# A four-layer hybrid encoder on one core: new layouts of input and result, one transfer for the small tensors, a new order in the first layer

## The chip, the cores and the metric

The kernel runs on 1 core of one Trainium2 chip. The metric is the device time of one execution in microseconds (us). Before the change the median of 3 runs is 1135.5 us (1133.83 to 1135.89).

A core has a matrix engine (TensorE: PE for its products, PEld for its weight loads), VectorE (DVE), ScalarE (ACT), GpSimd (POOL) and SyncE (SP), which only issues transfers here. Each engine works through its own instructions in a fixed order and waits for the others by semaphores. 16 DMA engines move the data; transfers are issued on the queue of SP or of ACT.

## The reference

x has 256 tokens of 1024 values. Four layers follow, each of them a token mixer and a squared-ReLU MLP with 4096 hidden values, each with an RMSNorm ahead of it and a residual sum behind it. Layers 0 and 3 mix by a diagonal complex state-space model (S5) with a gate, layer 1 by differential attention, layer 2 by pooling.

```python
for i in range(DEPTH):
    kind, j = i % N_MIXERS, i // N_MIXERS
    h = rmsnorm(x, norm_mix[i])
    if kind == 0:
        m = s5_mixer(h, s5_w_in[j], s5_lam_re[j], s5_lam_im[j], s5_log_step[j], s5_b_re[j], s5_b_im[j],
                     s5_c_re[j], s5_c_im[j], s5_d[j], s5_w_gate[j], s5_w_out[j])
    ...
    x = x + m.astype(x.dtype)
    h = rmsnorm(x, norm_mlp[i])
    x = x + sqrelu_mlp(h, mlp_w1[i], mlp_w2[i]).astype(x.dtype)
return rmsnorm(x, norm_final).astype(x.dtype)
```

The S5 mixer of a layer: u = h w_in; in each of 64 groups a recurrence over the tokens with 64 complex states, whose coefficients come from lam, step, b and c; y from the states plus d u; z = gelu(y); z times sigmoid(z w_gate); the product with w_out.

## The kernel before

The 256 tokens are two tiles (t = 0, 1) of 128 partitions; x stays in the on-chip memory for the whole run (start_x_1, start_x_2). Partition p of tile t holds token 128 t + 4 (p mod 32) + p // 32: four tokens that follow each other form a step of the recurrence, and their place s in the step is the slowest part of the partition's number. So the view of x and of the result in DRAM is "(t c s) d -> t s c d", with s = 4 outermost.

All weights come as 338 blocks of 128 x 1024 values in the order of their use (`load`, three buffers named raw). In most products a block is split into a rounded high part and a low part (whi by ScalarE, wlo by VectorE), and three products take the place of one. The first layer's input product (w_in) and the first of its gate blocks take the block as it is, in full precision.

In `s5` of layer 0 the order of the work is written by hand: SEQ[0] is a list of steps, each a letter and a number, and all engines keep to it. The letters that matter here:

- p: the parameters (dt, mag, a sine, the factors wa, wb, pa, pb), in seven pieces, small steps of VectorE, with copies on ScalarE for wb, pa and pb.
- f q t: transpose block q of x in tile t on TensorE, copy it out on ScalarE times the norm's weights (`first`). x: the norm's statistics (ScalarE, then GpSimd).
- g n: a quarter of the input product, 8 matrix products in full precision with one block of weights for one half of the input; V n reads it out and transposes it on VectorE.
- i, I, d, o, O, s, a, r: tables of a quarter (products of the coefficients s5bc with the factors on VectorE, copies on ScalarE); S: four transposes of the table; T, U: a small table from 16 products. Z: GpSimd clears a table.
- m, n, c, C, y, z: states in, transposition, recurrence on VectorE in two parts, output product and GELU, transposition of the quarter.
- e and w: the gate and the output product. From the last transposition (z) on the order of both versions is the same.

At the start (`build`) ScalarE's queue issues the unit matrix and the norm weights (ident, cols), SP's queue the parameters of the first layer (prm), x in four transfers of 256 KB, the first two blocks of weights, the first half of the coefficients (in_s5bc) and three small tensors (dskip, chunk, gmask). At most eight transfers are open: each later one waits until the one eight places ahead of it has landed.

At the end (`last`), for each tile, the second half of x gets the final norm: ScalarE sums squares, GpSimd makes 1/rms, ScalarE or VectorE scales, and SP stores the half row (line 1239).

## Time and profile before

| | before |
|---|---|
| median of 3 runs | 1135.5 us (1133.83 to 1135.89) |
| the profiled execution | 1133.78 us |
| its span, first to last instruction | 1132.0 us |
| TensorE busy | 1091.0 us (96%) |
| VectorE busy | 792.5 us (70%) |
| ScalarE busy | 661.6 us (58%) |
| GpSimd busy | 57.9 us (5%) |
| moved by DMA | 196.50 MB, mean 174 GB/s |

The span counts from the first to the last instruction; what the time has beyond it (1.8 us) lies around the execution. The rows below come from this one execution. In a timeline each row is a run of like instructions of one engine: start, duration, engine, line, operation, result <- operands, and in brackets how long the engine stood idle before it and what it waited for. A helper records most instructions, so that nearly all of them have line 106; they are told apart by their tiles. One product of full precision leaves two records.

### The profile page before, as it was taken

What the parts mean: (1) busy time and instruction counts of PE and PEld (TensorE: products, weight loads), DVE (VectorE), ACT (ScalarE), POOL (GpSimd) and SP (SyncE); (2) the same over time, 40 slices, a digit from 0 to 9 for tenths busy, and PEclk for the clock granted to TensorE, in tenths of its full rate; (3) what the DMA queues carried; (4) which work ended last, traced back from release to release, by engine and by line L of the source; (5) the groups of instructions that cost most, each with busy time, mean ns of one, the idle gap of its engine ahead of it and who ended that gap; (6) DMA issues with size and microseconds to landing.
All of it is one profiled execution on the core that took longest, in us unless ns stands there. A gap on an engine that the chain in (4) does not pass through costs nothing.

```text
span 1132.0 us, 18755 instructions
## 1 busy us (share of the span) xinstructions
PE 1091.0 (96%) x7128; PEld 965.0 (85%) x7128; DVE 792.5 (70%) x1464; ACT 661.6 (58%) x1314; POOL 57.9 (5%) x113
## 2 busy tenths in 40 slices
PE   5989999999999999999999999999998999999994
PEld 4878798999887888999898899988897889899883
DVE  8997699567668987967655865565569777555653
ACT  4797576556665676666545754454473366444542
POOL 2301010000010011000000200000010001000000
PEclk9999999999999999999999999999999999999997
DMA  5314477766664535667667366666655565666561
GB/s 160 113 38 125 155 198 235 231 196 220 198 183 147 167 113 186 209 201 216 189 190 231 95 190 187 184 183 189 186 167 150 164 189 172 194 188 186 174 190 51
DMA packets 56698, 196.50 MB, mean 174 GB/s; under 512 B 7200, under 2 KB 7712, under 8 KB 56608
## 3 DMA queue, kind: packets, MB, share of 16 engines
q1 hardware_dynamic: 54560, 189.70, 55.9%
q10 hardware_dynamic: 2048, 5.61, 1.4%
q8 instruction: 56, 0.92, 0.3%
q14 instruction: 34, 0.28, 0.1%
HBM read 188.46 MB, written 6.82 MB: 173 GB/s over the span
## 4 chain that ended last, share of the span: by engine, by line
PE 87%; DVE 7%; ACT 2%; DMA 2%; issue 1%; SPq 0%; POOL 0%; DVEq 0%; ACTq 0%; POOLq 0%
PE mlp_ps L169 65%; PE mix_ps L169 21%; DVE mix_m L106 6%; PE mix_ps L173 2%; DMA start_raw<-in_wts 1%; ACT start_T L106 1%; ACT mix_m L106 1%; ACT mlp_m L106 0%; PE mlp_ps L173 0%; DMA mix_raw<-in_wts 0%; DVE mix_wlo L106 0%; ACT mix_whi L106 0%; SPq L1139 0%; DVE mix_mx L106 0%; DVE mix_cad L106 0%
## 5 line engine op out<-in xcount | busy, mean ns | idle before, releaser
L106 DVE TENSOR_TENSOR mlp_wlo<-mlp_raw,mlp_whi 128x512 fp32r<-128x512 f32 x492 | 319.1, 687 | 216.2 <-ACT mlp_whi L106 215.9
L106 ACT CAST mlp_whi<-mlp_raw 128x512 fp32r<-128x512 f32 x492 | 282.1, 619 | 257.6 <-PE mlp_ps L169 201.8
L169 PE MATMUL mlp_ps<-mlp_whi,mlp_m 128*128 128x512 f32 x1024 | 327.8, 396 | 0.0
L169 PEld LDWEIGHTS mlp_ps<-mlp_whi,mlp_m 128*128 128x128 f32 x1024 | 192.8, 188 | 45.5
L169 PE MATMUL mlp_ps<-mlp_m,mlp_whi 128*128 128x256 f32 x1248 | 226.2, 283 | 0.0
L169 PE MATMUL mlp_ps<-mlp_wlo,mlp_m 128*128 128x512 f32 x512 | 202.9, 396 | 0.0
L169 PEld LDWEIGHTS mlp_ps<-mlp_m,mlp_whi 128*128 128x128 f32 x1248 | 192.1, 188 | 0.6
L169 PE MATMUL mlp_ps<-mlp_m,mlp_wlo 128*128 128x256 f32 x624 | 175.2, 281 | 0.0
L169 PE MATMUL mlp_ps<-mix_m,mlp_whi 128*128 128x256 f32 x672 | 122.1, 283 | 0.0
L169 PEld LDWEIGHTS mlp_ps<-mlp_m,mlp_wlo 128*128 128x128 f32 x624 | 118.3, 190 | 0.0
L169 PEld LDWEIGHTS mlp_ps<-mlp_wlo,mlp_m 128*128 128x128 f32 x512 | 96.5, 188 | 22.1
L169 PE MATMUL mix_ps<-mix_whi,mix_m 128*128 128x512 f32 (+1 forms) x352 | 106.6, 379 | 0.0
L169 PEld LDWEIGHTS mlp_ps<-mix_m,mlp_whi 128*128 128x128 f32 x672 | 104.5, 188 | 1.8
L106 DVE TENSOR_TENSOR mix_wlo<-mix_raw,mix_whi 128x512 fp32r<-128x512 f32 x124 | 80.8, 687 | 29.8 <-ACT mix_whi L106 29.7
L106 ACT CAST mix_whi<-mix_raw 128x512 fp32r<-128x512 f32 x124 | 71.8, 621 | 47.0 <-PE mix_ps L169 22.9
L169 PE MATMUL mlp_ps<-mix_m,mlp_wlo 128*128 128x256 f32 x336 | 94.5, 281 | 0.0
L169 PEld LDWEIGHTS mix_ps<-mix_whi,mix_m 128*128 128x128 f32 x352 | 64.3, 188 | 13.7 <-issue 0.9
L169 PE MATMUL mix_ps<-mix_wlo,mix_m 128*128 128x512 f32 (+1 forms) x176 | 66.0, 375 | 0.0
L106 DVE TENSOR_TENSOR mlp_m<-mlp_m,mlp_m 128x512 fp32r<-128x512 f32 (+1 forms) x72 | 51.7, 718 | 19.4 <-ACT mlp_m L106 19.3
L169 PEld LDWEIGHTS mlp_ps<-mix_m,mlp_wlo 128*128 128x128 f32 x336 | 63.8, 190 | 0.0
L106 ACT CAST mlp_m<-mlp_m 128x512 fp32r<-128x512 f32 x64 | 39.8, 622 | 23.0 <-DVE mlp_m L106 22.7
L106 DVE TENSOR_TENSOR mix_m<-mix_m,mix_m 128x512 f32<-128x512 f32 (+3 forms) x64 | 44.8, 727 | 5.6 <-ACT mix_m L106 4.9
(307 smaller groups left out, 1378.2 us busy)
## 6 DMA issues: line engine op xcount, KB each, us to landing
mlp_raw<-in_wts SPq DMA_DIRECT2D x252, 512.0 KB, 4.3
mix_raw<-in_wts SPq DMA_DIRECT2D x84, 512.0 KB, 4.5
kept<-mlp_m SPq DMA_DIRECT2D x4, 512.0 KB, 5.5
start_st<-kept SPq DMA_DIRECT2D x32, 64.0 KB, 4.3
start_x<-in_x SPq DMA_DIRECT2D x4, 256.0 KB
start_raw<-in_wts SPq DMA_DIRECT2D x2, 512.0 KB, 9.8
mlp_m<-in_s5bc SPq DMA_DIRECT2D x2, 512.0 KB
kept<-start_O ACTq DMA_DIRECT2D x4, 256.0 KB, 5.3
```

The lines of the kernel that those rows point to most:

```text
L106: i = f(*a, **k)
L169: i = self.nc.tensor.matmul(*a, **k)
L173: i = self.nc.tensor.transpose(*a)
```

## The change

1. x is passed as (tile, half, 128, 512) in the order of the partitions, so that each of the four loads reads 256 KB in one piece. The result is stored in the same layout, and put in order by the host afterwards, as x is put in order by the host ahead.
2. Six small tensors (the first layer's parameters, the unit matrix, the norm weights, chunk, dskip, gmask) become columns of one tensor of 128 x 426, loaded by one transfer on ScalarE's queue. The coefficients are issued ahead of the first weights.
3. SEQ[0], the order of the first layer, is another list of the same steps.

```diff
+OFFSET, SMALL = {}, 0
+for k, n in (("s5p", 96), ("ident", 128), ("cols", 72), ("chunk", 64), ("dskip", 64), ("gmask", 2)):
+    OFFSET[k] = SMALL, n
+    SMALL += n
...
-       0: "f00 p0 f01 p1 p1 p1 p1 p1 p1 i0 d1 g0 o1 f10 f11 d0 g1 s0 x01 o0 x00 x10 g0 I0 Z a0 r0 S0 x11 i1 V0 g1 Z g3 i3 V1 O0 Z Z m0 T0 n0 I1 s1 g2 T1 c0 a1 r1 U0 s2 i2 g2 V2 S1 g3 I3 d2 I2 C0 m1 S2 Z O1 o2 n1 c1 C1 y0 a2 z0 m2 U1 e0 d3 r2 s3 n2 c2 o3 V3 y1 S3 z1 a3 T2 e0 U2 C2 m3 O2 T3 r3 O3 n3 c3 U3 C3 e1 y2 e1 y3 z2 z3 e0 e0 e1 w0 e1 w0 w1 w0 w0 w1 w1 w1",
+       0: "p0 f00 p1 p1 p1 p1 d1 d0 p1 p1 f01 i1 f10 x00 Z x10 s0 g2 g0 x01 i0 i2 a0 r0 f11 I1 I0 x11 s1 g0 V0 g1 S1 a1 Z o1 g1 S0 m0 r1 Z Z o0 T0 n0 i3 O0 V1 I2 d2 T1 I3 c0 U0 m1 g3 g3 s2 C0 V3 Z S2 n1 O1 o2 a2 c1 y0 d3 g2 z0 S3 V2 e0 o3 O2 U1 C1 m3 m2 r2 s3 e1 n2 n3 c2 a3 C2 y1 z1 T2 U2 T3 r3 c3 O3 U3 C3 e1 y2 e0 y3 z2 z3 e0 e0 e1 w0 e1 w0 w1 w0 w0 w1 w1 w1",
...
-        xv = io["x"].rearrange("(t c s) d -> t s c d", t=NT, s=4)
-        self.ident = self.t([128, 128], "ident")
-        cols = self.t([128, 9, 8], "gcol")
-        self.prm = self.t([128, 3, 32], "prm", 1)
-        nc.scalar.dma_start(out=self.ident, in_=io["ident"])
-        nc.scalar.dma_start(out=cols, in_=io["cols"])
+        small = self.t([128, SMALL], "small")
+        nc.scalar.dma_start(out=small, in_=io["small"])
+        part = lambda k, p=128: small[0:p, OFFSET[k][0]:sum(OFFSET[k])]
+        self.prm = part("s5p").rearrange("p (a j) -> p a j", a=3)
+        self.ident, self.chunk = part("ident"), part("chunk")
+        self.gcol = cols = part("cols").rearrange("p (a j) -> p a j", a=9)
+        self.dsk = part("dskip", 32).rearrange("p (l j) -> p l j", l=2)
+        self.gmask = part("gmask", 32)
         for n in range(2):
             for t in range(NT):
-                if (n, t) == (0, 0):
-                    nc.sync.dma_start(out=self.prm, in_=io["s5p"][0])
-                nc.sync.dma_start(out=self.x[t][:, 512 * n:512 * n + 512], in_=xv[t, :, :, 512 * n:512 * n + 512])
-            self.load()
+                nc.sync.dma_start(out=self.x[t][:, 512 * n:512 * n + 512], in_=io["x"][t, n])
             if n == 0:
                 self.bc = self.m4([128, 4, 16, 16])
                 nc.sync.dma_start(out=self.bc, in_=io["s5bc"][0, 0])
-        self.gcol = cols
-        self.dsk, self.chunk = self.t([32, 2, 32], "dsk"), self.t([128, 64], "chunk")
-        self.gmask = self.t([32, 2], "gmask")
-        nc.sync.dma_start(out=self.dsk, in_=io["dskip"])
-        nc.sync.dma_start(out=self.chunk, in_=io["chunk"])
-        nc.sync.dma_start(out=self.gmask, in_=io["gmask"])
+            self.load()
...
-        ov = self.io["out"].rearrange("(t c s) d -> t s c d", t=NT, s=4)
         for n in range(2):
             y = self.y[t, n]
             if n and t:
                 self.ts(y, y, self.rstd[t], ALU.mult)
             else:
                 nc.scalar.activation(out=y, in_=y, func=AF.Copy, scale=self.rstd[t])
-            nc.sync.dma_start(out=ov[t, :, :, 512 * n:512 * n + 512], in_=y)
+            nc.sync.dma_start(out=self.io["out"][t, n], in_=y)
...
-    a["x"] = inp["x"][0]
+    a["x"] = inp["x"][0].reshape(NT, 32, 4, 2, 512).transpose(0, 3, 2, 1, 4).reshape(NT, 2, 128, 512)
...
+    small = np.zeros((128, SMALL), np.float32)
+    for k, (o, n) in OFFSET.items():
+        v = a["s5p"][0] if k == "s5p" else a.pop(k)
+        small[:len(v), o:o + n] = v.reshape(len(v), n)
+    a["small"] = small
...
-    io["out"] = nc.dram_tensor("out_y", (256, 1024), F32, kind="ExternalOutput").ap()
+    io["out"] = nc.dram_tensor("out_y", (NT, 2, 128, 512), F32, kind="ExternalOutput").ap()
...
-    return r.results[0]["out_y"].reshape(1, 256, 1024)
+    y = r.results[0]["out_y"].reshape(NT, 2, 4, 32, 512)
+    return np.ascontiguousarray(y.transpose(0, 3, 2, 1, 4)).reshape(1, 256, 1024)
```

On SP's queue the head before (raw: weights, start_m: the first half of the coefficients):

```order
L1138 DMA start_prm_67<-in_s5p 128x96
L1139 DMA start_x_1_63<-in_x 128x1x512
L1139 DMA start_x_2_64<-in_x 128x1x512
L214 DMA start_raw_73<-in_wts 128x1024
L1143 DMA start_m_7_75<-in_s5bc 128x1024
L1139 DMA start_x_1_63<-in_x 128x1x512
L1139 DMA start_x_2_64<-in_x 128x1x512
L214 DMA start_raw_79<-in_wts 128x1024
L1147 DMA start_dsk_81<-in_dskip 32x64
L1148 DMA start_chunk_82<-in_chunk 128x64
L1149 DMA start_gmask_83<-in_gmask 32x2
L214 DMA mix_raw_281<-in_wts 128x1024
```

and now:

```order
L1144 DMA start_x_1_63<-in_x 128x512
L1144 DMA start_x_2_64<-in_x 128x512
L1147 DMA start_m_4_69<-in_s5bc 128x1024
L219 DMA start_raw_71<-in_wts 128x1024
L1144 DMA start_x_1_63<-in_x 128x512
L1144 DMA start_x_2_64<-in_x 128x512
L219 DMA start_raw_75<-in_wts 128x1024
L219 DMA mix_raw_305<-in_wts 128x1024
L1017 DMA mix_rope_3633<-in_rope 128x128
L1019 DMA mix_mask_3635<-in_mask 128x128
L219 DMA mix_raw_307<-in_wts 128x1024
L566 DMA mix_m_106_340<-in_s5bc 128x1024
```

The four loads of x are 128 x 512, four small transfers are gone from this queue, and the second half of the coefficients (mix_m<-in_s5bc) stands as the twelfth, behind the fourth block of weights.

On ScalarE at the start, from the copy-out of the first transposed block of x on (mix_q_sc is the sine, mix_q_wb, pa and pb the factors, mix_cad copies of coefficients):

```order
L106 ACTIVATE mix_m_24_104<-mix_ps_105,start_gcol_66 128x128 x4
L106 ACTIVATE mix_m_24_104<-mix_ps_149,start_gcol_66 128x128 x4
L106 ACTIVATE mix_q_sc_118<-mix_q_a_193 128x64
L106 ACTIVATE mix_q_wb_240<-mix_q_wa_239 128x32x4
L106 COPY mix_q_wb_240<-mix_q_wa_239 128x32x4
L106 COPY mix_q_pa_241<-mix_q_pr_119 128x4x32
L106 ACTIVATE mix_q_pa_241<-mix_q_pi_120 128x4x32
L106 ACTIVATE mix_q_pb_242<-mix_q_pi_120 128x4x32
L106 ACTIVATE mix_q_pb_242<-mix_q_pr_119 128x4x32
L106 COPY mix_cad_277<-start_m_7_75 128x8x16
L106 ACTIVATE mix_cad_277<-start_m_7_75 128x8x16
```

and now, from the sine on, which follows the copy-out of the first block:

```order
L111 ACTIVATE mix_q_sc_98<-mix_q_a_174 128x64
L111 COPY mix_cad_220<-start_m_4_69 128x8x16
L111 ACTIVATE mix_cad_220<-start_m_4_69 128x8x16
L111 COPY mix_cad_223<-start_m_4_69 128x8x16
L111 ACTIVATE mix_cad_223<-start_m_4_69 128x8x16
L111 ACTIVATE mix_q_wb_227<-mix_q_wa_226 128x32x4
L111 COPY mix_q_wb_227<-mix_q_wa_226 128x32x4
L111 COPY mix_q_pa_228<-mix_q_pr_99 128x4x32
L111 ACTIVATE mix_q_pa_228<-mix_q_pi_100 128x4x32
L111 ACTIVATE mix_q_pb_229<-mix_q_pi_100 128x4x32
L111 ACTIVATE mix_q_pb_229<-mix_q_pr_99 128x4x32
L111 ACTIVATE mix_m_34_129<-mix_ps_259,start_small_65 128x128 x4
```

The second copy-out (mix_m_34<-mix_ps_259) has moved from ahead of the sine to behind the factors.

On TensorE the head before (x4: the transposes of a block of x; x8: a quarter product with one block of weights):

```order
L173 MATMUL mix_ps_105<-start_ident_65,start_x_1_63 128x128 x4
L173 MATMUL mix_ps_149<-start_ident_65,start_x_2_64 128x128 x4
L169 MATMUL mix_ps_280<-start_raw_73,mix_m_24_104 128x256 x8
L173 MATMUL mix_ps_301<-start_ident_65,start_x_1_63 128x128 x4
L173 MATMUL mix_ps_310<-start_ident_65,start_x_2_64 128x128 x4
L169 MATMUL mix_ps_322<-start_raw_79,mix_m_24_104 128x256 x8
L169 MATMUL mix_ps_280<-mix_raw_281,mix_m_92_300 128x256 x8
```

and now:

```order
L178 MATMUL mix_ps_130<-start_small_65,start_x_1_63 128x128 x4
L178 MATMUL mix_ps_259<-start_small_65,start_x_2_64 128x128 x4
L178 MATMUL mix_ps_274<-start_small_65,start_x_1_63 128x128 x4
L174 MATMUL mix_ps_304<-start_raw_71,mix_m_34_129 128x256 x8
L174 MATMUL mix_ps_319<-start_raw_75,mix_m_34_129 128x256 x8
L178 MATMUL mix_ps_354<-start_small_65,start_x_2_64 128x128 x4
L174 MATMUL mix_ps_319<-mix_raw_305,mix_m_82_273 128x256 x8
L174 MATMUL mix_ps_398<-mix_raw_307,mix_m_34_129 128x256 x8
```

The third transposed block comes ahead of the first product, the fourth behind the second, and the first two products are for two different quarters.

## Rows read from the trace of the kernel before

**Rows 1.** The page: busy time, share of the span and instructions of each engine.
```profile
PE 1091.0 (96%) x7128; PEld 965.0 (85%) x7128; DVE 792.5 (70%) x1464; ACT 661.6 (58%) x1314; POOL 57.9 (5%) x113
```

**Rows 2.** Stretches: length, busy us (instructions) of PE, PEld, DVE, ACT, POOL; PEclk, DMA share, GB/s.
```profile
6.00:7.00 1.00, 0.00 (x0) 0.00 (x0) 0.86 (x5) 0.00 (x0) 0.00 (x0) 1.00 1.07 256
...
17.00:18.00 1.00, 1.00 (x7) 0.85 (x6) 0.90 (x9) 0.98 (x5) 0.00 (x0) 1.00 0.26 100
...
40.00:60.00 20.00, 19.71 (x152) 16.79 (x150) 19.71 (x23) 16.26 (x27) 2.96 (x5) 1.00 0.26 81
...
182.00:183.00 1.00, 1.00 (x11) 1.00 (x10) 1.00 (x2) 0.36 (x1) 0.00 (x0) 1.00 1.07 426
```

**Rows 3.** Stretches at the end of the span, same columns.
```profile
1117.00:1118.00 1.00, 0.00 (x0) 0.00 (x0) 0.92 (x2) 1.00 (x3) 0.00 (x0) 1.00 0.00 0
...
1118.00:1119.00 1.00, 0.00 (x0) 0.00 (x0) 0.00 (x0) 0.14 (x2) 0.70 (x2) 0.84 0.22 25
...
1126.00:1127.00 1.00, 0.00 (x0) 0.00 (x0) 0.00 (x0) 0.00 (x0) 0.00 (x0) 0.50 0.26 102
...
1130.00:1131.00 1.00, 0.00 (x0) 0.00 (x0) 0.00 (x0) 0.00 (x0) 0.00 (x0) 0.50 0.07 27
```

**Rows 4.** Timeline of the end: start, us, engine, line, operation, operands, idle before.
```profile
1116.94 4.03 SPq L1239 DMA_DIRECT2D out_y<-mlp_m  x4
...
1119.07 0.52 DVE L106 TENSOR_SCALAR mlp_m<-mlp_m,mlp_rs 128x512 f32<-128x512 f32 x1 [1.12 <-POOL mlp_rs L106]
...
1119.07 0.72 ACT L106 ACTIVATE mlp_m<-mlp_m,mlp_rs 128x512 f32<-128x512 f32 x1 [0.93 <-POOL mlp_rs L106]
```

**Rows 5.** DMAs of the tile kept: us from issue to landing.
```profile
DMA to landing us min/median/max: 2.3/4.8/6.0
```

**Rows 6.** Timeline of the start, VectorE and ScalarE.
```profile
0.73 0.41 ACTq L106 DMA_DIRECT2D start_ident<-in_ident  x1
...
2.71 0.18 DVE L106 TENSOR_SCALAR mix_q_lr<-start_prm 128x32 f32<-128x32 f32 x1 [1.78 <-DMA start_prm<-in_s5p]
...
12.30 1.15 ACT L106 ACTIVATE mix_m<-mix_ps,start_gcol 128x128 f32<-128x128 f32 x4 [2.17 <-PE mix_ps L173]
...
13.62 0.19 DVE L106 TENSOR_TENSOR mix_q_pr<-mix_q_mag,mix_q_sc 128x32 f32<-128x32 f32 x1 [1.77 <-ACT mix_q_sc L106]
...
18.10 1.22 DVE L106 TENSOR_TENSOR mix_m<-start_m,mix_q_wa 128x1024 f32<-128x1024 f32 x1
...
18.12 0.44 ACT L106 ACTIVATE mix_q_pb<-mix_q_pr 128x128 f32<-128x128 f32 x1
```

**Rows 7.** Timeline of the start, TensorE.
```profile
7.86 1.09 PE L173 MATMUL mix_ps<-start_ident,start_x 128*128 128x128 f32 x4 [7.86 <-DMA start_x<-in_x]
...
12.49 5.51 PE L169 MATMUL mix_ps<-start_raw,mix_m 128*128 128x256 f32 x16 [0.23 <-DMA start_raw<-in_wts]
...
21.24 3.72 PE L169 MATMUL mix_ps<-start_raw,mix_m 128*128 128x256 f32 x16 [0.57 <-DMA start_raw<-in_wts]
...
28.25 1.91 PE L173 MATMUL mix_ps<-start_ident,start_ba 128*128 128x128 f32 x16
```

**Rows 8.** DMAs of the tile mix_raw: us from issue to landing.
```profile
DMA to landing us min/median/max: 3.6/5.0/10.2
```

**Rows 9.** Timeline of the first layer: waits of ScalarE and TensorE, one slow step of VectorE.
```profile
34.54 1.21 ACT L106 ACTIVATE mix_m<-mix_ps,mix_rs 128x256 f32<-128x256 f32 x3 [2.13 <-POOL mix_rs L106]
...
48.35 2.56 DVE L106 TENSOR_SCALAR mix_m<-mix_m 128x512 f32<-128x512 f32 x1
...
48.83 1.80 POOL L106 MEMSET start_O<- 128x2048 f32 x1
...
65.34 0.65 PE L173 MATMUL mix_ps<-start_ident,mix_m 128*128 128x128 f32 x4 [1.47 <-ACT mix_m L106]
...
74.56 0.44 PE L169 MATMUL mix_ps<-start_T,mix_m 128*64 128x128 f32 x4 [0.94 <-ACT start_T L106]
...
102.67 1.42 PE L173 MATMUL mix_ps<-start_ident,mix_m 128*128 128x128 f32 x8
```

## The prediction

> **What bounds the kernel now.** I read the page first: TensorE is busy for 96% of the span [rows 1]. Nothing that shortens only another engine's work can gain much in the middle, and the change leaves the middle alone: apart from names, the instructions of all engines differ only in the first layer's mixer (the first 105 us) and in the four stores of the result. So I looked at the two ends, in stretches of 1 us.
>
> At the end, TensorE's last product is over by 1116.5, the last values that are to be stored are ready at 1119.07 + 0.52 = 1119.59 (VectorE) and 1119.07 + 0.72 = 1119.79 (ScalarE) [rows 4], and yet the span runs to 1132.0. Between 1120 and 1130 no engine works, and the stores move 102 GB/s at a DMA share of 0.26 [rows 3]. A share of 0.26 that never changes means that about 4 of 16 DMA engines run. The loads of x at the start show the same, 0.26 and 100 GB/s [rows 2], while other traffic reaches a share of 1.07 and 256 to 426 GB/s [rows 2]. The old view of x and of the result has four tokens of a chunk as its outermost dimension, and so cuts each transfer in four; the new layout is 128 rows of 2 KB.
>
> At the start, TensorE waits for x until 7.86 and for the first weights until 12.49 [rows 7]. From 20 us on both TensorE and VectorE are busy for 19.7 us in 20 [rows 2]: the first layer has two limits at the same time, and a gain on one of them alone is worth nothing.
>
> **The change part by part. The stores.** Before: 4 x 256 KB = 1.05 MB at 102 GB/s take 10.3 us, from about 1119.8 to 1130.3 [rows 3], and the span ends 1.7 us later. Now the first two stores, issued from 1116.94 on, are out of the way before the last two, which can issue at about 1119.6 and 1120.0 [rows 4]. First bytes follow 1.2 us after an issue (1116.94, and nothing in the stretch of 1117, traffic in that of 1118 [rows 3, 4]), so at 1120.8. The last two are 0.52 MB; at 400 GB/s, between the best row and a little less [rows 2], they need 1.3 us: 1122.1, and with the same 1.7 us behind them the span ends at 1123.8, **8.2 us** earlier. Bounds: a store that lands 2.3 us after its issue, the fastest of the tile kept, ends at 1122.3 and the span at about 1123.2 (-8.8); one that needs 6.0 us, the slowest, and that amid weight loads, lands at 1126.0, and the span ends at about 1126.5 (-5.5) [rows 5]. I stay at the fast end, since no weights are in flight then.
>
> **Loads and the small tensor.** The parameters of the first layer came alone, 48 KB, and VectorE began at 2.71 [rows 6]. Now they lie in a tensor of 128 x 426 values, 218 KB, beside 256 KB of x: 0.48 MB at 256 to 426 GB/s [rows 2] are 1.1 to 1.9 us, after first bytes at about 1.9 (ScalarE's first issue stood at 0.73 [rows 6], and 1.2 us behind it, as above). I take a landing at 3.8, so +1.1. Bounds: 2.7 (nothing lost) and 7.9, when x landed before [rows 7]. Against it, the sine on ScalarE stood behind the eviction of the second block of x (12.30 to 13.45), and VectorE lost 1.77 us there [rows 6]; in the new order only the first block stands ahead of the sine, and that wait goes. VectorE reaches the table products at 18.1 + 1.1 - 1.8 = 17.4.
>
> **The new order on ScalarE and TensorE.** The eviction of the second block now stands behind the six copies of the table factors, which wait for VectorE and ended at 18.12 + 0.44 = 18.56 [rows 6]; with VectorE 0.7 earlier, at 17.9. So the second half of TensorE's first product waits until about 18.2, although its weights are there by about 9 (1.8 MB stand in the queues up to them, at 256 GB/s, after 1.9); before, that product began at 12.49. The profile's clock column says 1.00 from the start, but the first 16 records of this shape took 5.51 us and the next 3.72 [rows 7]; I read the lower level, 1.2 GHz, for the first 1.8 x 2 = 3.6 us, and expect it once more after a pause of some 7 us. TensorE then needs 1.8 (half a product) + 1.8 (the low level) + 3.6 + 0.6 (a transpose) + 3.6 = 11.4, and has three products done at 29.6; before, at 28.25 [rows 7]. That is **+1.35**.
> A rule bears on the 1.8: the Trainium skill, "TensorE: Matmul & The Clock Gate", section "Part 1: The HAM clock gate (the "warmup" mystery)", says that an array left idle drops to the half rate and has to earn the full one again. The first row agrees (5.51 against 3.72); no run here shows what a pause of 7 us does. By the rule the +1.35 stands; without it the term is -0.45.
> Later TensorE loses 3.6 us in three waits (the first, 1.47, and the last, 0.94, stand in [rows 9]) where the read-out of one quarter stands right behind the step that it needs. In the new order a product of 3.6 us stands before the first of these transposes, four transposes before the gate product, and several steps before the third: **-3.6**. New waits: the first output step for VectorE's chain (I get 1.1), the second transposition for a function table and the GELU (0.7 to 1.5): together **+2.0**, bounds 0.5 and 4. TensorE: 1.35 - 3.6 + 2.0 = -0.2.
>
> **The same on VectorE.** It starts the products 0.7 early. The second half of the coefficients (in_s5bc) now stands on SP's queue behind a weight load that waits until TensorE is done with the first weights (21.8): issued at 22.2, landed by the median 5.0 us later, 27.2 [rows 8]; VectorE wants it after two table groups of three products of 1.2 us [rows 6] and a small one of half that, at 17.4 + 3.6 + 1.8 + 3.6 = 26.4: **+0.8**, bounds 0 (3.6) and 6.0 (10.2). Before the first transposition, ScalarE has two evictions, three statistics, a table, a third eviction and four copies to do, and then waits for GpSimd as it did for 2.13 us [rows 9]: it lets VectorE wait about 1.3, against 0.6 before, and about 1.0 more at the next quarter, **+1.7**; two waits of 0.5 near the end go, **-1.0**. One step of VectorE took 2.56 us, not 0.43, while GpSimd cleared start_O [rows 9]; in the new order the same three instructions meet again, so nothing changes. VectorE: -0.7 + 0.8 + 1.7 - 1.0 = +0.8.
>
> The two engines meet at the last output step, which needs both. Between -0.2 and +0.8 I take **+0.3** for the first layer, bounds -3 (clock up, no collision, small tensor early) and +4. Sum on the profiled execution: span 1132.0 - 8.2 + 0.3 = 1124.1. That execution took 1133.78, near the fastest of the three timed ones, whose median is 1135.5; I take the difference from the median: 1135.5 - 7.9 = **1127.6**.
>
> **Rivals.** (a) *The first layer gains as well.* If the pause does not lower the clock (-1.8), and GpSimd's clearing does not meet VectorE's step (-2.1), both engines come forward by about 2 to 4: 1124.5. For it: both rows are single events; against it: both engines have to gain together. (b) *The eviction behind the table factors costs more.* If the small tensor lands at 5 to 6 instead of 3.8, VectorE, hence that eviction, hence TensorE all shift, 1 for 1, and the coefficients too: +3, 1130.6. (c) *The stores are not spread.* If the end stays at 4 engines, nothing is gained there: 1135.8. For it only that no row shows a store of this very shape alone; against it every load of 128 rows in rows 2. The Trainium skill, "DMA: Bandwidth & Descriptors", section "Why a DMA increments its semaphore by 16 and not by 1", says that the engines of a transfer are the largest number up to 16 that divides the slowest dimension of both sides; 4 before, 16 now. The trace agrees for 4 (0.26). (d) *Slower than before*: the coefficients stuck on SP's queue. VectorE stops at 26.4 until they land, and everything behind follows. To eat the 8 us and 2.3 more they have to land after 37, 15 us after their issue; the longest weight load took 10.2 [rows 8]. Worked out at 15 us: 26.4 becomes 37.2, and 1135.5 - 8.2 + 10.8 = 1138.1.
>
> **How the numbers follow.** Forecast (stores 8, first layer within 1.5 either way) 0.50; (a) 0.22; (b) 0.18; (c) 0.07; (d) 0.03. A measurement of this kernel can tell about 0.2%, 2.3 us: faster means below 1133.2. Forecast, (a) and (b) are faster, 0.90; (c) is the same, 0.07; (d) slower, 0.03. The range leaves out (c), (d) and the far parts of (a) and (b), and takes in the -5.5 of the slow store: 1123.4 to 1131.0.
>
> **What would show it.** In the new profile the stretches behind the last product should show a DMA share near 1, not 0.26, and about 7 us from the last issue to the end should be gone; if the share is 0.26, (c) holds. x and the weights should be there by 11 us. TensorE's first product should be cut in two, with a pause up to 18, and its 16 records should take long again; ScalarE should show the second block's eviction at about 18. VectorE should lose no time before the table products, a little at the second coefficients and 1 us or more at the first two transpositions, and the transposition behind the last output step should start within 1.5 us of 102.67, where it was [rows 9]. A start at 99 to 100 means (a), at 105 to 106 (b). The forecast is wrong if the middle moves: from there on no order differs.

## The result, and the profile after

The changed kernel takes **1120.4 us** (median of four runs, 1119.85 to 1120.80), the kernel before 1135.6 us in the same comparison: a ratio of 0.987, 95% interval 0.985 to 0.989. The forecast was 1127.6, its range 1123.4 to 1131.0: the sign is right, the gain about twice what was forecast. The profiled executions take 1120.8 and 1133.78 us, with spans of 1119.0 and 1132.0. Those 13.0 us fall into three pieces, cut at two points that both traces have: the start of the eight transpositions behind the last output step (z) and the end of TensorE's last product.

| | before | after | difference | forecast |
|---|---|---|---|---|
| first layer, up to z | 102.67 | 103.61 | +0.9 | +0.3 |
| middle, z to the end of the last product | 1013.8 | 1008.6 | **-5.2** | 0 |
| end, last product to the end of the span | 15.6 | 6.8 | -8.8 | -8.2 |

**The page** of the changed kernel, which answers to [rows 1]: busy time, share and instructions of each engine.

```profile
PE 1086.3 (97%) x7128; PEld 963.6 (86%) x7128; DVE 793.0 (71%) x1464; ACT 658.4 (59%) x1312; POOL 52.8 (5%) x113
```

TensorE runs as many instructions as before and is busy for 4.7 us less. No step removes products; they have become shorter.

**The end**, in stretches of 1 us, as in [rows 3] (columns: length, busy us of PE, PEld, DVE, ACT, POOL, PEclk, DMA share, GB/s):

```profile
1113.00:1114.00 1.00, 0.00 (x0) 0.00 (x0) 0.70 (x2) 0.95 (x3) 0.00 (x0) 1.00 0.41 152
1114.00:1115.00 1.00, 0.00 (x0) 0.00 (x0) 0.12 (x1) 0.12 (x1) 0.82 (x3) 1.00 0.98 369
...
1116.00:1117.00 1.00, 0.00 (x0) 0.00 (x0) 0.00 (x0) 0.00 (x0) 0.00 (x0) 0.76 0.74 277
1117.00:1118.00 1.00, 0.00 (x0) 0.00 (x0) 0.00 (x0) 0.00 (x0) 0.00 (x0) 0.50 0.67 248
```

The timeline there, as in [rows 4]:

```profile
1111.82 0.40 PE L174 MATMUL mlp_ps<-mlp_whi,mlp_m 128*128 128x512 f32 x1
...
1112.75 3.48 SPq L1237 DMA_DIRECT2D out_y<-mlp_m  x4
...
1114.88 0.72 ACT L111 ACTIVATE mlp_m<-mlp_m,mlp_rs 128x512 f32<-128x512 f32 x1 [0.93 <-POOL mlp_rs L111]
1114.88 0.52 DVE L111 TENSOR_SCALAR mlp_m<-mlp_m,mlp_rs 128x512 f32<-128x512 f32 x1 [1.15 <-POOL mlp_rs L111]
```

The first two stores go out at a DMA share of 0.98 while the last values are still being worked out; the last two follow at 0.74 and 0.67, where the share stood at 0.26 for ten microseconds. From the last value (1114.88 + 0.72) to the end it is 3.4 us. The last product of the kernel before, with whose end the table's last row begins:

```profile
1116.04 0.40 PE L169 MATMUL mlp_ps<-mlp_whi,mlp_m 128*128 128x512 f32 x1
```

**The start**: the timeline of TensorE, which answers to [rows 7]:

```profile
4.51 1.97 PE L178 MATMUL mix_ps<-start_small,start_x 128*128 128x128 f32 x8 [4.51 <-DMA start_small<-in_small]
...
9.78 3.62 PE L174 MATMUL mix_ps<-start_raw,mix_m 128*128 128x256 f32 x8
18.60 8.22 PE L174 MATMUL mix_ps<-start_raw,mix_m 128*128 128x256 f32 x24 [5.20 <-ACT mix_m L111]
...
27.10 7.07 PE L174 MATMUL mix_ps<-mix_raw,mix_m 128*128 128x256 f32 x32
```

And those of VectorE and of ScalarE, which answer to [rows 6]:

```profile
4.50 0.18 DVE L111 TENSOR_SCALAR mix_q_lr<-start_small 128x32 f32<-128x32 f32 x1 [3.57 <-DMA start_small<-in_small]
...
18.00 1.22 DVE L111 TENSOR_TENSOR mix_m<-start_m,mix_q_wa 128x1024 f32<-128x1024 f32 x1
```

```profile
12.53 0.26 ACT L111 ACTIVATE mix_q_sc<-mix_q_a 128x64 f32<-128x64 f32 x1 [5.71 <-DVE mix_q_a L111]
...
18.23 2.12 ACT L111 ACTIVATE mix_m<-mix_ps,start_small 128x128 f32<-128x128 f32 x8
```

Stretches with the granted clock around TensorE's pause (the column behind POOL):

```profile
14.00:15.00 1.00, 0.00 (x0) 0.00 (x0) 1.00 (x11) 0.00 (x0) 0.00 (x0) 1.00 0.00 0
18.00:19.00 1.00, 0.40 (x1) 0.40 (x2) 1.00 (x2) 1.00 (x6) 0.00 (x0) 0.50 0.00 0
...
22.00:23.00 1.00, 1.00 (x3) 0.76 (x3) 0.96 (x2) 0.18 (x2) 1.00 (x1) 0.50 0.00 0
24.00:25.00 1.00, 1.00 (x6) 0.86 (x5) 1.00 (x2) 0.41 (x1) 0.99 (x1) 0.87 0.81 262
```

The first product is cut in two, as forecast (one product leaves two records, so its first half is the row at 9.78). TensorE waits from 13.40 to 18.60 for ScalarE's eviction of the second block, and works at the lower level (0.50, 1.2 GHz) until about 24.

**The middle.** Where do 5.2 us go when no order differs? Set against each other instruction by instruction, the two traces show no single place where time is won: the changed kernel gains some 0.35 us in every 72 us, and nothing only between some 800 and 920 us, around layer 3's mixer. The two costliest groups of products of the MLP show it too (group: tiles, form, count | busy us, mean ns of one). Before:

```profile
L169 PE MATMUL mlp_ps<-mlp_whi,mlp_m 128*128 128x512 f32 x1024 | 327.8, 396 | 0.0
...
L169 PE MATMUL mlp_ps<-mlp_m,mlp_whi 128*128 128x256 f32 x1248 | 226.2, 283 | 0.0
```

After:

```profile
L174 PE MATMUL mlp_ps<-mlp_whi,mlp_m 128*128 128x512 f32 x1024 | 326.1, 395 | 0.0
...
L174 PE MATMUL mlp_ps<-mlp_m,mlp_whi 128*128 128x256 f32 x1248 | 225.0, 282 | 0.0
```

The mean of one is its length with its way through the engine; consecutive products overlap. What counts is the time from one start to the next, worked out from the start times in the trace: over all products with split weights (whi, wlo) between 160 and 1100 us, 233.96 ns before and 232.35 after for 512 columns (some 2000 products), 120.00 and 119.44 for 256 (some 3240). Some records are missing; with the intervals beside them left out the four figures are 234.16 and 232.53, 119.88 and 119.25, so they hold to about 0.2 ns and their differences better. 2000 x 1.6 + 3240 x 0.56 ns = 5.0 us: all of the middle's gain.

What does differ there are addresses, worked out from the sizes of the tiles. A tile's memory is laid out in the order in which the tiles are first used, and the merged small tensor and the new place of the weight load shift two pools: the twelve activation tiles (m4) start at byte 26432 of a partition instead of 38176, the raw weights at 75584 instead of 25888. The split weights stay at 201920. So the experiments start there.

### The profile page after: what moved, and what is told of

It reads as the page before. It is cut to its first block, busy times and chain, and to the rows that moved or that the text cites. A ratio compares the mean times of both kernels' runs of the same rounds, so it can differ in the third digit from the quotient of the medians.

```text
span 1119.0 us, 18753 instructions
## 1 busy us (share of the span) xinstructions
PE 1086.3 (97%) x7128; PEld 963.6 (86%) x7128; DVE 793.0 (71%) x1464; ACT 658.4 (59%) x1312; POOL 52.8 (5%) x113
## 4 chain that ended last, share of the span: by engine, by line
PE 87%; DVE 8%; ACT 3%; issue 1%; DMA 1%; POOL 0%; DVEq 0%; ACTq 0%; POOLq 0%
PE mlp_ps L174 65%; PE mix_ps L174 20%; DVE mix_m L111 6%; PE mix_ps L178 2%; ACT mix_m L111 1%; ACT start_T L111 1%; ACT mlp_m L111 0%; DVE mix_ex L111 0%; PE mlp_ps L178 0%; DMA mix_raw<-in_wts 0%; DMA start_small<-in_small 0%; DVE mix_wlo L111 0%; ACT mix_whi L111 0%; ACT L111 0%; ACT start_st L111 0%
## 5 line engine op out<-in xcount | busy, mean ns | idle before, releaser
L111 ACT CAST mlp_m<-mlp_m 128x512 fp32r<-128x512 f32 x64 | 39.7, 620 | 23.2 <-DVE mlp_m L111 23.1
```

Of the source, the lines that this page charges most:

```text
L111: i = f(*a, **k)
```

## The experiments

Four explanations of the middle stood against each other: theory A (the start addresses), B (the order of the first layer, or the moment at which it hands over), C (the transfers: fewer small ones, other neighbours), and for the first layer D and E (the merge, or the new order, costs it time).

**e1 and e2: addresses alone, in either kernel.** e1 adds 32 unused bytes ahead of the raw weights and the activations of the kernel before, and 32 behind them, so that both start at multiples of 64; e2 adds the same in the changed kernel, where both started at multiples of 64 and now no longer do.

```diff
-        cols = self.t([128, 9, 8], "gcol")
+        cols = self.t([128, 80], "gcol")[:, 0:72].rearrange("p (a j) -> p a j", a=9)
...
-        self.dsk, self.chunk = self.t([32, 2, 32], "dsk"), self.t([128, 64], "chunk")
+        self.dsk, self.chunk = self.t([32, 72], "dsk")[:, 0:64].rearrange("p (a j) -> p a j", a=2), self.t([128, 64], "chunk")
```

```diff
-        small = self.t([128, SMALL], "small")
+        small = self.t([128, SMALL + 8], "small")[:, 0:SMALL]
...
-        self.mhalf, self.hpi = self.t([128, 1], "mhalf"), self.t([128, 1], "hpi")
+        self.mhalf, self.hpi = self.t([128, 9], "mhalf")[:, 0:1], self.t([128, 1], "hpi")
```

> The kernel before with nothing moved but addresses: 32 unused bytes ahead of the raw weight tiles and the twelve activation tiles (m4), and 32 behind them, so that these fifteen tiles start at multiples of 64 bytes in a partition's memory (25920 and 38208, where they started at 25888 and 38176, 32 over one), and every other tile keeps its remainder. No instruction and no order differs. Theory A (addresses): TensorE takes the MLP's products faster when the activations start at a multiple of 64; the group of 1024 products of 128x512 from mlp_whi goes from 396 to about 395 ns, its busy time from 327.8 to 326.1 us, the last product ends about 5 us earlier (1111.4 after 1116.4) and the time is 1130.5 us. Theory B (order and moment: the middle runs faster since the first layer hands over in another order or at another moment): nothing changes, 1135.5 us. Theory C (transfers: fewer small ones on the queue, other neighbours for the later ones): nothing changes, 1135.5 us.

> The changed kernel with 32 unused bytes behind the merged small tile and 32 in the tile of a constant behind the raw weights: raw weights and activations start 32 over a multiple of 64 again, as in the kernel before; everything else keeps its remainder, and no instruction or order differs. Theory A (addresses): the middle loses what it had gained, 1120.4 + 5.0 = 1125.4 us, the 1024 products of mlp_whi back at 327.8 us busy. Theories B (order and moment) and C (transfers): 1120.4 us, 326.1 us busy.

Measured: e1 1125.2 us, a ratio to before of 0.992 (0.990 to 0.993); e2 1124.9 us. The same shift takes 9.9 us from the one and adds 4.5 us to the other. The groups of e2, and the two rows that bound its middle:

```profile
L174 PE MATMUL mlp_ps<-mlp_whi,mlp_m 128*128 128x512 f32 x1024 | 327.8, 396 | 0.0
...
L174 PE MATMUL mlp_ps<-mlp_m,mlp_whi 128*128 128x256 f32 x1248 | 226.2, 282 | 0.0
```

```profile
102.67 1.42 PE L178 MATMUL mix_ps<-start_small,mix_m 128*128 128x128 f32 x8
...
1115.78 0.40 PE L174 MATMUL mlp_ps<-mlp_whi,mlp_m 128*128 128x512 f32 x1
```

They are back at the 327.8 and 226.2 us of before, and its middle takes 1013.5 us, the middle of before (1013.8), with the changed kernel's order, layouts and transfers. So B and C fall: the 5 us come from addresses. But e1 gained twice what theory A in its first form gave it (9.9, not 5), so the form was wrong.

**e5 and e4: which remainder?** e5 moves the S5 layers' tiles (ba, st, O, T) by 32 bytes, and what lies behind them, the split weights among it, by 64; e4 moves all behind the merged tensor by 64 (`SMALL + 16` in the line of e2).

```diff
-        self.mhalf, self.hpi = self.t([128, 1], "mhalf"), self.t([128, 1], "hpi")
+        self.mhalf, self.hpi = self.t([128, 9], "mhalf")[:, 0:1], self.t([128, 1], "hpi")
...
-        self.subln = self.t([128, 4], "subln")
+        self.subln = self.t([128, 12], "subln")[:, 0:4]
```

> The changed kernel with 32 more bytes ahead of the S5 layers' tiles (ba, st, O, T), which in both kernels start 32 over a multiple of 64, and 32 behind them: now all tiles that TensorE reads start at a multiple of 64. Theory A (addresses): the products that read them come closer to each other too, but they are few (some 290 of 7128, and 128x128 products of ba show 59.5 ns from start to start in both kernels): between -1 and 0 us, 1119.4 to 1120.4 us. Theories B and C: 1120.4 us.

> The changed kernel with 64 unused bytes behind the merged small tile: all later tiles 64 bytes further on. Activations and raw weights go from 64 over a multiple of 128 to a multiple of 128, the split weights (whi, wlo) too; the S5 layers' tiles stay 32 over a multiple of 64. No instruction differs. Theory A, remainder of 64 alone: 1120.4 us. Theory A, remainder of 128 of the weights too, as the two shifted kernels suggest (256-column products from start to start in 117.7 ns with the weights at a multiple of 128, 119.5 with the weights 64 over): some 3000 products by 1.8 ns, less some 0.9 ns on 1900 products of 512 columns, so about -3.5 us, 1116.9 us. Theory B: 1120.4 us.

Measured: e5 1114.3 us, 6 us faster than the changed kernel, where at most 1 was expected; e4 1120.1 us, no change, where multiples of 128 should have given 3.5. Neither the remainder by 64 nor that by 128 of a start explains both. What e4 leaves as it was, and e1 and e5 change, is the distance from the activations to the split weights.

**m1 and m2: TensorE alone.** Nothing but products in the kernel's pattern of three, for pairs of starts:

```diff
+        for n in (512, 256):
+            for a, b in [(0, 0)] + LINE + FINE:
+                combo(a, b, n)
```

> Nothing of the network: one row of input is split into a high and a low part, and TensorE alone then multiplies them, 36 products for each pair of start addresses, in the kernel's pattern of three (high by high, high by low, low by high, each with its own weight load), 512 and then 256 columns wide. The stationary part (a) and the moving part (b) start 0, 32, 64, ... 224 bytes over a multiple of 256, all 64 pairs; then 4, 8, ... 28 bytes for one of them, the other at 0. No other engine works meanwhile. Theory A1 (the start addresses of TensorE's own two operands set the pace): the time from start to start differs by pair as in the kernels, about 234.1 ns where the stationary part of a 512-column product starts 32 or 96 over, 232.4 where both start 64 over, 233.3 where one starts 64 over and the other 0; 120.0, 119.5 and 117.7 ns for 256 columns. Theory A2 (the addresses matter only through other engines' use of the same memory): all pairs show the same interval. Theory B (order and moment): the same too.

> As in the run of 64 pairs of start addresses, TensorE alone, 36 products a case, but with the stationary part always at a multiple of 256 and the moving part 0, 4, 8, ... 508 bytes further, 512 and then 256 columns wide. In that run the interval followed the difference of the two starts (moving less stationary) and not either of them: 226.6 or 226.7 ns at 0, 228.9 at 64, 233.3 to 234.4 elsewhere for 512 columns; 113.3 ns at 192, 117.2 to 120.1 elsewhere for 256. Theory F (the difference, with a period of 256 bytes): the second half of the scan repeats the first, and the multiples of 32 give the same values again. Rival (the difference without that period, or the place of each tile as well): the second half differs.

m1 answers with a pattern that no single address explains: the interval is nearly the same along each diagonal of the 8 x 8 table, 226.6 to 226.7 ns for 512 columns wherever both parts start alike, whether at 0 or at 224. A few cells stand apart: at a difference of 128 one reads 232.4 where the others read 233.5, and at 192, 256 columns wide, one reads 117.8 where seven read 113.3; m3 comes back to that. It is the **difference** of the two starts that counts, moving less stationary. m2 scans it in steps of 4 bytes; its second half repeats the first within 0.04 ns, so the period is 256 bytes. The stretches of m2 at a difference of 0 and of 192, 256 columns wide, show it in the counts (3 us each; the first number in brackets counts the products):

```profile
1098.00:1101.00 3.00, 3.00 (x27) 3.00 (x27) 0.00 (x0) 0.00 (x0) 0.00 (x0) 1.00 0.02 5
1304.00:1307.00 3.00, 3.00 (x29) 3.00 (x28) 0.00 (x0) 0.00 (x0) 0.00 (x0) 1.00 0.00 0
```

From start to start, ns, worked out from the start times of 27 products each:

| moving less stationary, bytes | 0 | 32 | 64 | 96 | 128 | 160 | 192 | 224 | over all steps of 4 |
|---|---|---|---|---|---|---|---|---|---|
| 512 columns | 226.7 | 233.4 | 228.9 | 233.3 | 233.5 | 234.3 | 233.2 | 233.4 | 226.7 to 240.0 |
| 256 columns | 120.0 | 116.5 | 117.8 | 119.9 | 118.6 | 117.4 | 113.3 | 118.4 | 113.3 to 123.2 |

No other engine works in these runs, so A2 falls as well. In the network the weights move in the products of 512 columns and stand still in those of 256 (but for 240 of the latter, layer 3's input product, whose weights move: 118.6 ns in the changed kernel and 119.7 in e11, which has d = 0, where the table has 118.6 and 120.0 at their d). With d for weights less activations, the first read the table at d and the second at 256 - d. The kernel before has d = 160, as e2 has: 234.3 and 119.9 by the table, 233.9 and 120.0 in the kernels. The changed kernel and e4 have 128 (233.5 and 118.6; 232.4 and 119.5 in the kernels, and 232.4 is the cell of m1 that stood apart), e1 and e5 have 192 (233.2 and 117.8; 233.2 and 117.3 to 117.9). That is theory F, and it names a better d than any kernel had, the best of all steps of 4 for the two widths together: 64, with 228.9 and 113.3.

**e11, e9, e10: the difference chosen.** e11 brings d to 0 with 128 unused bytes (`[128, 33]` for the first constant); e9 and e10 bring it to 64 without a byte, since the activation tiles are given their place before the small ones. e9 on the changed kernel:

```diff
+        self.bc = self.m4([128, 4, 16, 16])
         small = self.t([128, SMALL], "small")
...
             if n == 0:
-                self.bc = self.m4([128, 4, 16, 16])
                 nc.sync.dma_start(out=self.bc, in_=io["s5bc"][0, 0])
```

> The changed kernel with 128 unused bytes behind the raw weights: the split weights start 64 over a multiple of 256 like the activations, difference 0. Theory F: the 2000 products of 512 columns go from 232.5 to 226.7 ns (-11.6 us), the 2880 of 256 columns from about 119.5 to 120.0 ns (+1.4 us): 1110 us; the 1024 products of mlp_whi shorter while those of 256 columns are not. Theory A in its first form (all starts stay at multiples of 64): 1120.4 us.

> The changed kernel with the activation tiles given their place ahead of the merged small tensor: they start 128 over a multiple of 256, the split weights stay at 192 over, so that weights less activations is 64 and activations less weights 192, the best pair of the scan together. No instruction, no order differs. Theory F (the difference of the two start addresses sets the pace): some 2000 products of 512 columns go from 232.5 to 228.9 ns (-7.2 us), 2880 of 256 columns from about 119.5 to 113.3 ns (-17.9 us): 1120.4 - 25 = 1095 us, unless the splitting of the weights or their transfers become late, which would show as waits of TensorE. Theory A in its first form (multiples of 64, or of 128, of each start): 1117 to 1120.4 us.

> The kernel before with the layouts of x and the result alone, and with the activation tiles given their place first, which makes weights less activations 64 here too. Theory F: against the layouts alone (1123.1 us) some 2000 products of 512 columns go from 234.1 to 228.9 ns (-10.4 us) and 2880 of 256 columns from 120.1 to 113.3 ns (-19.6 us): 1093 us. And if the merge and the new order cost the first layer what the four kernels with either say (1.3 us each), this one lies some 2 us below the changed kernel with its activation tiles first. Theory A in its first form: 1117 to 1120 us.

Measured: e11 1112.7 us (ratio to before 0.981), e9 **1100.2** (0.971, 0.969 to 0.972), e10 1099.8 (0.970, 0.969 to 0.972; its runs spread from 1098.1 to 1102.4). The groups of e11:

```profile
L174 PE MATMUL mlp_ps<-mlp_whi,mlp_m 128*128 128x512 f32 x1024 | 320.7, 390 | 0.0
...
L174 PE MATMUL mlp_ps<-mlp_m,mlp_whi 128*128 128x256 f32 x1248 | 226.1, 283 | 0.0
```

And of e9:

```profile
L174 PE MATMUL mlp_ps<-mlp_whi,mlp_m 128*128 128x512 f32 x1024 | 323.2, 392 | 0.0
...
L174 PE MATMUL mlp_ps<-mlp_m,mlp_whi 128*128 128x256 f32 x1248 | 215.3, 277 | 0.0
```

In e11 the products of 512 columns became shorter and those of 256 did not, as F said and a rule of multiples cannot say; e9 has both. The gains are 7.7 of 10.2 us, 20.2 of 25, and 23.2 of 30 expected: the mechanism holds, its size was put a fifth to a quarter too high. One reason stands in the intervals: e9 has 229.5 and 114.6 ns on the mean, not 228.9 and 113.3.

**m3, e12, e13: the two paces.** In e10's trace the products of 256 columns follow each other in about 113.6 ns in some stretches (240 to 280 us, 460 to 600) and in 117.8 in others (180 to 220, and nearly all behind 620), at one and the same d. m3 asks TensorE, with nothing beside it but short copies by ScalarE, what sets that; e12 and e13 move the raw weights' start in e10 and e9, which differ in it (below m3's loops stands the edit of e12; e13 has `SMALL + 8` in place of its first pair of lines).

```diff
+        for target in (16, 32, 48, 24):
+            for prior in range(0, 64, 8):
+                run(prior, 256, 36)
+                run(target, 256, 72)
...
+        for target in (48, 32):
+            for wait in range(16):
+                nc.scalar.copy(g[:, 0:128 + 4 * wait], bank[0][:, 0:128 + 4 * wait])
+                run(target, 256, 72, g[:, 0:128])
```

```diff
-        cols = self.t([128, 9, 8], "gcol")
+        cols = self.t([128, 80], "gcol")[:, 0:72].rearrange("p (a j) -> p a j", a=9)
...
-        self.mhalf, self.hpi = self.t([128, 1], "mhalf"), self.t([128, 1], "hpi")
+        two = self.t([128, 2], "mhalf")
+        self.mhalf, self.hpi = two[:, 0:1], two[:, 1:2]
```

> TensorE alone again, 72 products of 256 columns at one of four differences (moving less stationary 64, 128, 192 and 96 bytes), each time behind something else: 36 products of 256 columns at each of eight differences, 24 of 512 columns at each of eight; then, for 192 and 128, behind a pause in which TensorE waits for a copy of 128 to 188 columns by ScalarE, sixteen lengths. Theory G (the entry chooses between paces): one difference shows more than one pace over these entries, 113.3 and 117.8 ns among them for 192, and the pace then lasts. Rival H (TensorE alone has one pace for a difference, and what disturbs it in the kernels is other engines' work): each difference shows one value, 117.8 at 64, 118.7 at 128, 113.3 at 192, 120.1 at 96.

> The kernel before with the layouts alone, the activation tiles first, and now the raw weights moved by 32 bytes to a multiple of 64 (75072, were at 75040); two constants share a tile so that all else stays in place. No order differs. If the raw weights' start has a part in TensorE's pace: its 256-column products keep 113.3 to 113.8 ns behind 620 us too, where they stood at 117.8, and the time is 1096 us, with little spread. If it has none (the difference of TensorE's own operands alone, with two paces that something else chooses): 1098 to 1102 us as without the move. By either, the first layer keeps its 2 us over the changed kernel.

> The changed kernel with its activation tiles first, and the raw weights moved by 32 bytes to 32 over a multiple of 64; two constants share a tile, so all else stays in place. If the raw weights' start has a part: the 256-column products fall to 117.8 ns in some stretches and the time goes from 1100.1 to 1104 us or more. If it has none: 1100 us.

m3: theory G. At a difference of 192 the 72 products follow each other in 113.3 ns behind 22 of 32 entries and in 117.8 behind the other ten (at 113.3 behind ten of the sixteen entries with a copy by ScalarE, at 117.8 behind six); at 64 it is 113.3 behind four of 16 and 117.8 behind twelve, at 128 118.6 or 120.0, at 96 about 120.0 behind all 16. The pace of products 6 to 30 of a stretch is also that of its last 30, so it lasts. The copies were meant to make TensorE pause, and hardly did: they run beside the products ahead of them, and the first two products of these stretches follow their predecessors in 112 to 165 ns (once in 330 and 226), where 113 to 123 is usual. So a delay of some 50 ns or less, or one product with weights from another place (the copy), can change the pace. At 128, behind nine such entries in a row that delayed nothing, the pace stayed at 120.0 through all nine stretches. Two stretches of 7 us at a difference of 192, behind entries that differ by 4 columns of ScalarE's copy:

```profile
898.00:905.00 7.00, 7.00 (x64) 7.00 (x64) 0.00 (x0) 0.00 (x0) 0.00 (x0) 1.00 0.01 2
907.00:914.00 7.00, 7.00 (x62) 7.00 (x61) 0.00 (x0) 0.00 (x0) 0.00 (x0) 1.00 0.00 0
```

That also says why the kernel before was so even, at 120.0 ns: its 256-column difference is 96, with one pace.

e13: 1100.1 us, as e9. e12: **1097.7 us** (1097.0 to 1099.4), e10 having had 1099.8; the intervals in its trace still change from 113.6 to 117.8 behind some 900 us, and e13's do too (it loses 3.3 us on e9 behind 920 us, and had gained about as much by then, 2.5 of it between 843 and 920). The raw weights' start has no part that shows, and the 2.1 us by which e12 lies below e10 are within what the two paces scatter. They are also why e10 does not lie 2 us below e9, as was expected of its sooner first layer: its middle takes 992.9 us in the profiled execution (1102.4 us, its slowest), e9's 988.3. e12 is the fastest version of this study: a ratio to before of 0.968 (0.966 to 0.969), 23 us faster than the changed kernel. Its page:

```profile
PE 1066.4 (97%) x7128; PEld 948.8 (87%) x7128; DVE 791.4 (72%) x1464; ACT 660.0 (60%) x1314; POOL 57.4 (5%) x113
```

It has neither the merge nor the new order, which the next three runs account for.

**e3, e6, e8: the three parts apart.** e3 is the kernel before with the layouts of x and the result alone; e8 adds the new order to it; e6 is the changed kernel with the old order. For e3 the lines on x, on the result and on the host's layout of the diff above were taken over, for example:

```diff
-                nc.sync.dma_start(out=self.x[t][:, 512 * n:512 * n + 512], in_=xv[t, :, :, 512 * n:512 * n + 512])
+                nc.sync.dma_start(out=self.x[t][:, 512 * n:512 * n + 512], in_=io["x"][t, n])
...
-            nc.sync.dma_start(out=ov[t, :, :, 512 * n:512 * n + 512], in_=y)
+            nc.sync.dma_start(out=self.io["out"][t, n], in_=y)
```

For e6 and e8 the one line of the table of orders that the change replaces was put back, or taken over.

> The kernel before with one part of the change alone: x and the result laid out in the order of their transfers. Order of the first layer, small tensors and all addresses as before. The prediction's step for the stores: 15.6 us between the last product and the end become 6.8, so -8.8 us, 1126.8 us. Theory A (addresses) and theory B (order and moment) add nothing to that: the last product ends at 1116.4 in the span, as before, or a few tenths earlier for the x transfers. Theory C (transfers) lets the middle gain up to 5 us more: 1121.8 us.

> The changed kernel with the first layer in the old order: layouts and merged small tensor stay, and the activations stay at their changed address. The layouts alone had the first layer over 2.0 us sooner than before, the changed kernel 0.8 us later, so that merge and order together take 2.8 us. Theory D (the merge takes them: one small transfer that lands later): 1120.4 us. Theory E (the new order takes them): 1117.6 us. By the prediction's own steps, the order gives 0.2 us to TensorE and the merge takes 1.1 on the landing: 1120.6 us. Theory A (addresses): the MLP's products at the changed kernel's pace, 326.1 us busy for the 1024 of mlp_whi.

> The kernel before with the layouts and the new order of the first layer, but the small tensors apart, and so activations and raw weights at the old addresses. Theory D (the merge takes the first layer's 2.8 us): 1123.1 us as with the layouts alone. Theory E (the new order takes them): 1125.9 us. Theory A (addresses): the middle at the pace of before in both cases, 327.8 us busy for the 1024 products of mlp_whi. Theory B (order and moment): the middle 5 us faster with the new order, 1118.1 to 1120.9 us.

Measured: e3 1123.1 us (0.990, 0.989 to 0.992), e6 1119.4 (0.988), e8 1124.3 (0.991). Where the address changes the middle, the first layer has to be read by itself, at z. In the timeline of TensorE, e3, then e8, then e6, then the changed kernel:

```profile
100.72 1.42 PE L173 MATMUL mix_ps<-start_ident,mix_m 128*128 128x128 f32 x8
```

```profile
102.08 1.42 PE L173 MATMUL mix_ps<-start_ident,mix_m 128*128 128x128 f32 x8
```

```profile
102.37 1.42 PE L178 MATMUL mix_ps<-start_small,mix_m 128*128 128x128 f32 x8
```

```profile
103.61 1.42 PE L178 MATMUL mix_ps<-start_small,mix_m 128*128 128x128 f32 x8
```

From 102.67 [rows 9] the layouts take 1.95 us; the new order adds 1.36, the merge (with its addresses) 1.65, and both together 2.89. Each figure is from one execution, and in the six other kernels with the merge and the new order (e2, e4, e5, e9, e11, e13) z stands at 102.48 to 103.02, so that both together cost 1.8 to 2.9 us. So D and E are both right by half: the order and the merge each cost the first layer about 1.5 us, and the layouts hide most of that.

One step of VectorE shows most of what the new order costs. In the changed kernel GpSimd clears another tile (start_ba) just when VectorE takes a step that took it 0.43 us before:

```profile
22.25 1.58 DVE L111 TENSOR_SCALAR mix_m<-mix_m 128x512 f32<-128x512 f32 x1
```

```profile
21.75 1.80 POOL L111 MEMSET start_ba<- 128x2048 f32 x1
```

It takes 1.58 in e8 too, and 0.43 in e3 and e6, with the old order: 1.15 us, where e8 lies 1.36 behind e3. No run moves that clearing alone, so that it is the cause of the 1.36 is argued and not shown.

And the middles answer theory A once more: 1013.4 in e3 and e8, with the old addresses, and 1008.4 in e6, with the new ones, whatever the order.

All kernels, by d (weights less activations, modulo 256); intervals over the products with split weights between 160 and 1100 us, the middle from z to the last product's end, us:

| kernel | d | 512 columns, ns | 256 columns, ns | middle, us | time, us |
|---|---|---|---|---|---|
| before | 160 | 234.0 | 120.0 | 1013.8 | 1133.7 to 1135.6 |
| e3 / e8 / e2 | 160 | 233.9 | 120.0 | 1013.4 / 1013.4 / 1013.5 | 1123.1 / 1124.3 / 1124.9 |
| changed / e6 / e4 | 128 | 232.3 to 232.4 | 119.4 to 119.5 | 1008.6 / 1008.4 / 1008.8 | 1120.4 / 1119.4 / 1120.1 |
| e1 / e5 | 192 | 233.2 | 117.9 / 117.3 | 1005.0 / 1003.2 | 1125.2 / 1114.3 |
| e11 | 0 | 227.2 | 120.1 | 1001.8 | 1112.7 |
| e10 / e12 | 64 | 229.4 | 116.7 / 115.4 | 992.9 / 989.0 | 1099.8 / 1097.7 |
| e9 / e13 | 64 | 229.5 / 229.4 | 114.6 / 115.3 | 988.3 / 988.3 | 1100.2 / 1100.1 |

Four kernels with d = 160 have the same middle within 0.4 us, three with d = 128 too, however they differ otherwise.

## Why the prediction was wrong, point by point

**The middle (the step that failed).** "[...] the change leaves the middle alone: apart from names, the instructions of all engines differ only in the first layer's mixer [...] and in the four stores of the result." That compared which instructions stand in which order, and not where their operands lie. The sum's term for the middle, 0, was -5.2 us: d went from 160 to 128. e2, which brings d back to 160 with nothing but unused bytes, brings the middle back to 1013.5, and its time, 1124.9, lies inside the stated range. No rival had it either: all four took place in the first layer or at the end. The prediction had said what would prove it wrong, "if the middle moves", and no bound of the range stood for it.

The Trainium skill, "SBUF — State Buffer", section "A bandwidth-pool intuition that's wrong (but worth ruling out)", gives TensorE a second, independent read port for the weight load; by that alone the distance of the two operands would not matter. m1 and m2 show otherwise: 226.7 to 240.0 ns for 512 columns by distance, with nothing else at work. Where inside the chip the two meet, no run shows.

**The stores: right.** Forecast -8.2, bounds -8.8 and -5.5; measured -8.8 (15.6 to 6.8), and in e3, with nothing else changed, 15.6 to 7.0. The share behind the last product is 0.98 at its best, not 0.26, as rival (c) would have had it. The first two stores were out of the way before the last two, as the sum had assumed.

**The merged small tensor: the direction right, the size low.** It landed at 4.50, not 3.8 (+1.8, not +1.1, on 2.71 [rows 6]). ScalarE's sine no longer stands behind an eviction, so VectorE's wait of 1.77 is gone, as forecast; VectorE reaches the table products at 18.00, not at 17.4. Price at the end of the first layer, by e6 against e3: 1.65.

**ScalarE and TensorE: right in each step, low in one.** Second eviction 18.23 (forecast 17.9), second half of the first product 18.60 (18.2), the clock at 0.50 behind the pause. The pause was 5.20, not about 7, and the low level cost more: 24 records (a product and a half) took 8.22 us where 24 of 0.226 (7.07 for 32 at the full level gives 0.221, 3.62 for 16 in e3 gives 0.226) make 5.4, so 2.8 instead of 1.8. Three products were done at about 30.6 (half of the 7.07 behind 27.10), forecast 29.6. The three old waits, 3.6 us, are gone. Of the new waits, TensorE lost 0.80 at the first output step (forecast 1.1) and 1.16 at the second transposition (0.7 to 1.5).

**VectorE: right but for the coefficients and one collision.** No wait for them (forecast +0.8); 0.27 + 0.70 and 1.27 at the first transpositions (forecast 1.3 and 1.0); the collision with GpSimd's clearing stayed, 2.52 us after 2.56 [rows 9]. That a second clearing would meet an earlier step (1.58 after 0.43) had no term.

**The first layer: right in sum, and by luck.** +0.9 against +0.3, within the stated 1.5 us of 102.67. But it hides two misses of opposite sign: the x layout had no term of its own beyond "x and the weights should be there by 11 us", and it was worth 1.95; order and merge, which the sum had near zero together, cost 2.9 here.

**The sum.** -8.2 + 0.3 = -7.9 was forecast, and -13.0 stands between the two profiled executions: -0.6 from the stores, +0.6 from the first layer, and the whole rest, -5.2, from the middle. The medians differ by 15.2, since the profiled execution of before lay 1.8 us under its median, that of the changed kernel 0.4 over it.

## What to carry to other kernels

Where TensorE is the bound, two programs with the same instructions in the same order are not yet the same: compare the addresses of its operands as well, and work out the time from start to start of its products, since a uniform 0.5% shows in no list of waits. A short run of TensorE alone gives the best distance of the two operands, though a scan shows only one of the paces where there are two; here one moved line was worth 20 us, more than the change. And when several small transfers are merged, the most urgent one waits for all of them: price its landing, not the number of transfers.

## What the runs showed of the hardware that was not expected

- The pace of a stream of products, each with its own weight load, follows the distance of the two operands' starts in a partition's memory, with a period of 256 bytes: 226.7 to 240.0 ns for 512 columns, 113.3 to 123.2 for 256 (m2). The best distance differs by width (0 for 512; 112, 144 and 192 for 256).
- At some distances TensorE has two paces (113.3 and 117.8 ns at 64 and 192; 118.6 and 120.0 at 128), the entry into the stretch picks one, with a delay of 50 ns or less or with none that shows, and it lasts at least until the stretch ends (m3). What it is in the entry that decides, in time or in state, stays open, and with it how to hold the faster one in a kernel: e9, e12 and e13 have stretches of both.
- The Trainium skill, "TensorE: Matmul & The Clock Gate", section "Back-to-back issue gap", gives N / 2.4 + 2.5 ns between isolated products at the full clock, an estimate of 215.8 for 512 columns and 109.2 for 256. The best distances come to 226.7 and 113.3, the worst stand 24 and 14 ns above that estimate. The page also says that in a stream the spacing is set by the weight load too, which fits an interval that depends on where the weights lie; its figure for such a stream, 131 ns for 512 columns, is not borne out here, where no distance came below 226.7.
- Behind a pause of 3.4 us (e8, where TensorE waited from 13.52 to 16.95) the granted clock stood at 0.50, as behind the 5.2 us of the changed kernel:

```profile
17.00:18.00 1.00, 1.00 (x3) 0.82 (x4) 1.00 (x2) 1.00 (x5) 0.00 (x0) 0.50 0.00 0
```
